# Splitting the second output projection of a tile in three, with the transposes of an earlier tile ahead of the last piece

## The chip, the cores and the metric

The kernel runs on one core of one Trainium2 chip. The metric is the device time of one execution in microseconds (us); the median of the runs is given. The core has five engines that matter here: TensorE (PE, matmuls and transposes), VectorE (DVE), ScalarE (ACT), GpSimd (POOL) and the queue of SyncE (SP), which issues nearly all DMAs.

## The reference, cut to what matters

A trunk of two layers works on two request groups (256 and 512 rows, D_MODEL = 1024). Each layer has a token mixer (layer 0: windowed attention with sinks; layer 1: differential attention) and a SwiGLU channel mixer, each between two RMS norms:

```python
for i in range(DEPTH):                        # DEPTH = 2
    h = rms_norm(x, norm_mix_pre[i])
    m = mixer(h)                              # ends with  o @ w_o   (1024 x 1024)
    x = x + rms_norm(m, norm_mix_post[i])
    h = rms_norm(x, norm_ffn_pre[i])
    x = x + rms_norm(swiglu(h, ffn_w_gate_up[i], ffn_w_down[i]), norm_ffn_post[i])
```

The change lies where a mixer ends and its SwiGLU begins: the product with `w_o`, the norm after it, the residual add, the norm before the SwiGLU, and the transposes that give the SwiGLU its operands. This place occurs twice, once in each layer.

## The kernel before, in words

The 768 rows are six tiles of 128 (0 and 1 are the prompt, 2 to 5 the sample). Every float32 product is made of three matmuls on a high and a low part (`product_steps`, L306; the matmuls are L315, L316 and L317; L316 and L317 need one low part each). The high part is an ACT copy, the low part a DVE subtraction: `split` (L303, L304) for activations, `two_parts` (L222, L223) for weights. Weights come through a ring of five split buffers; `free` and `take` (L291, L298) split the next unit as soon as a buffer is free, and issue the loads (`wraw`, L196, on SP's queue) behind it.

`project` (L737) makes the second 512 columns of the output projection. For a tile t, `out_unit` (L541) is a list of steps: eight products (k = 0 to 7, three matmuls each) into one PSUM bank, then `project_end` (L552): ACT squares and sums the bank (L559), DVE multiplies it by the gain into `o[t]` (L560). For tile 5, the last, four releases of weight buffers stand between the products, one after every second (`releasing`, L325), so its list has 13 entries and that of the others nine. `half` cuts the list in two pieces; both are called by `staged` (L499).

`staged` goes over the tiles in the order 0, 3, 1, 2, 4, 5. For a tile the four stages of `finish` (L458) follow its projection: a, the reciprocal root of the row norm (ACT L359, POOL L360); b, the residual add (DVE L472), the row norm of the sum (ACT L365, L359, POOL L360) and the store of x (SP, L476); c, the scaled tile y (DVE L369); d, `combine` (L420): eight transposes on PE (L433, bank tp_h) and the splits out of their banks (ACT L303, DVE L304). For tiles 0, 1 and 2, stage d splits the two banks and copies them to `o` (ACT L442). For tiles 3, 4 and 5 it also forms the operands s1 to s4 of the SwiGLU's Strassen-like product (L447 to L457), which makes eight DVE and five ACT instructions. In an iteration the order is: first piece of the tile's projection, stage c of the tile two steps before, stage b of the tile one step before, second piece, stage d of the tile two steps before, stage a of the tile itself. Stages a to c are issued with high priority.

The five stages that are left over for tiles 4 and 5 are called by `ffn` (L940), in the order c of 4, b of 5, two products (`p1`, L963, bank px), d of 4, more products (p2), c of 5, two more p1, d of 5, and so on; then p4 (bank pz), p6 (py, with s2), p5 (pw, with s1). The first px matmul reads the high part of tiles 0, 1 and 2, the second (L316) their low part. The combinations of gate and up weights (L257 to L261) run on DVE from there on.

The order in which an engine runs its instructions is fixed when the program is built: the tile framework orders by priority (the order of the calls above, high priority first) among the instructions whose inputs it expects to be ready. In the trace each engine's instructions stand in the order of its list.

Of the kernel before, what the change touches and what calls it, by code (L numbers as in the profile page):

```python
# [19 lines left out]
KT = D // P  # L20
# [11 lines left out]
NT = 6  # L32
# [14 lines left out]
def trunk(  # L47
# [93 lines left out]
    raw_src, units = [], []  # L141
# [149 lines left out]
    def take(n):  # L291

        i = state["used"]
        state["used"] += n
        prepare(i + n)
        return [parts.pop(j) for j in range(i, i + n)]
# [97 lines left out]
    def load_x(sub, t):  # L394
        x = xpool.tile([P, D], F32, tag="x", name=f"x{sub}_{t}")
        nc.sync.dma_start(out=x, in_=x_at[sub][t])
        return x
# [60 lines left out]
    def finish(sub, t, o, ssy, x, g, comb):  # L458

        r = {}
        m, (ss, y) = o[t], ssy

        def stage_a():
            with tc.high_priority():
                r[0] = rstd(ss[:, 1:2], ss[:, 0:1], f"post{sub}_{t}")

        def stage_b():  # L470
            with tc.high_priority():
                state["add"] = nc.vector.scalar_tensor_tensor(  # L472
                    out=x, in0=m, scalar=r[0], in1=x, op0=ALU.mult, op1=ALU.add)
                if g is not None:
                    r[1] = row_rstd(x, y, f"pre{sub + 1}_{t}")
            nc.sync.dma_start(out=x_at[sub + 1][t], in_=x)  # L476

        def stage_c():
            with tc.high_priority():
                scaled(y, x, r[1], g)  # L480

        def stage_d():
            if comb is not None:
                combine(y, t, f"h{sub + 1}_{t}", comb, o)
                return
            for s in transposes(y, t, f"h{sub + 1}_{t}"):
                s()

        return [stage_a, stage_b] + ([stage_c, stage_d] if g is not None else [])

    def last_tile(sub, t, m, ssy, x, r):

        halves = [slice(0, 512), slice(512, 1024)]
        for c, q in zip(halves, (nc.sync, nc.scalar)):
            nc.vector.scalar_tensor_tensor(
                out=x[:, c], in0=m[:, c], scalar=r, in1=x[:, c], op0=ALU.mult, op1=ALU.add)
            q.dma_start(out=x_at[sub + 1][t][:, c], in_=x[:, c])

    def staged(sub, units, o, sq, g, comb=None):  # L499

        st = []
        for i, t in enumerate((0, 3, 1, 2, 4, 5) if comb is not None else range(NT)):
            x = load_x(sub, t)
            units[t][0]()
            if i >= 2 and g is not None:
                st[i - 2][2]()
            if i >= 1:  # L510
                st[i - 1][1]()
            units[t][1]()
            if i >= 2 and g is not None:
                st[i - 2][3]()
            if g is None and t == NT - 1:
                last_tile(sub, t, o[t], sq[t], x, sq["last"])
                break
            st.append(finish(sub, t, o, sq[t], x, g, comb))
            st[i][0]()
        if g is None:  # L520
            return []
        return [st[NT - 2][2], st[NT - 1][1], st[NT - 2][3], st[NT - 1][2], st[NT - 1][3]]
# [15 lines left out]
    def column_blocks(taken, width):  # L538
        return [tuple(w[:, j * width:(j + 1) * width] for w in s) for s in taken for j in range(2)]

    def out_unit(t, wk, o, n2, gp, sq, name):  # L541

        pm = bank(name)
        steps = product_steps(pm, [(htile(t, k), wk[k]) for k in range(KT)])
        if t == NT - 1:
            steps = releasing(steps, 4)
        return steps + [lambda: project_end(t, pm, o, n2, gp, sq, name)]  # L550
# [16 lines left out]
    def mixer_a(gp, g_next, first_steps, o):  # L567
        with ExitStack() as st:
# [164 lines left out]
            for s in att[:2] + fill[:2] + att[2:4] + fill[2:4] + att[4:] + fill[4:6] + [lambda: split_o(NT - 1)] + fill[6:]:  # L733
                s()
        return project(o, 0, 0, None, gp, g_next, wk_o, sq, LAG + 1)

    def project(o, layer, sub, turn_o, gp, g_next, wk, sq, done):  # L737
        gs = ExitStack()
        gpool2 = gs.enter_context(tc.tile_pool(name=f"comb{layer}", bufs=1, side="right", reuse_waits="tile"))
        comb = {  # L740
            n: tuple(gpool2.tile([P, 4, HALF], F32R, name=f"{n}{part}_{layer}") for part in ("hi", "lo"))
            for n in ("s1", "s2", "s4")}
        for t in range(done, NT):
            if turn_o is not None and t + 1 < NT:
                for s in turn_o(t + 1):
                    s()
            for s in out_unit(t, wk, o, 0, gp, sq, f"po{layer}_0_{t}"):
                s()
        wk = column_blocks(take(4), 512)
        units = {}  # L750
        for t in range(NT):
            steps = []

            def half(i, t=t, steps=steps):
                if i == 0:
                    steps += out_unit(t, wk, o, 1, gp, sq, f"po{layer}_1_{t}")
                n = len(steps) // 2
                for s in (steps[:n] if i == 0 else steps[n:]):
                    s()

            units[t] = [lambda half=half: half(0), lambda half=half: half(1)]
        return staged(sub, units, o, sq, g_next, comb), comb, gpool2, gs


    def mixer_b(gp, g_next, first_steps, o):
        with ExitStack() as st:
# [168 lines left out]
            for s in run:  # L935
                s()
        return project(o, 1, 2, lambda t: turn_o[t][1:], gp, g_next, wk_o, sq, 3)


# [539 lines left out]
```

## Time and profile before

| | us |
|---|---|
| median of 3 runs | 1687.86 |
| lowest and highest run | 1686.98, 1690.11 |
| the profiled execution's own time | 1688.34 |
| its span, first to last instruction | 1686.6 |
| PE busy in it | 1659.1 (98%) |
| DVE, ACT, POOL busy | 1251.3, 949.7, 81.7 |

The time of the profiled execution exceeds its span by 1.7 us, which lie around the instructions. Times in the rows count from the start of the span. The stage of layer 0 lies at about 262 to 341 us, that of layer 1 at about 1155 to 1234 us. The granted clock (PEclk) is TensorE's clock as a share of full speed; its mean over the span is 0.997.

### The profile page before, as it was taken

What the parts mean: (1) busy time and instruction counts of PE and PEld (TensorE: products, weight loads), DVE (VectorE), ACT (ScalarE), POOL (GpSimd) and SP (SyncE); (2) the same over time, 40 slices, a digit from 0 to 9 for tenths busy, and PEclk for the clock granted to TensorE, in tenths of its full rate; (3) what the DMA queues carried; (4) which work ended last, traced back from release to release, by engine and by line L of the source; (5) the groups of instructions that cost most, each with busy time, mean ns of one, the idle gap of its engine ahead of it and who ended that gap; (6) DMA issues with size and microseconds to landing.
All of it is one profiled execution on the core that took longest, in us unless ns stands there. A gap on an engine that the chain in (4) does not pass through costs nothing. (4 is left out here: it accounts for less than half of the span.)

```text
span 1686.6 us, 25513 instructions
## 1 busy us (share of the span) xinstructions
PE 1659.1 (98%) x9483; PEld 1514.3 (90%) x9483; DVE 1251.3 (74%) x2488; ACT 949.7 (56%) x2158; POOL 81.7 (5%) x104
## 2 busy tenths in 40 slices
PE   7999999999999999999999999999899999999998
PEld 7888878899999998888999999988799999998887
DVE  7888766896766666988777676874997666666886
ACT  6777775654444444556566666674744444444553
POOL 1000001000000000001000000331000000000001
PEclk9999999999999999999999999999999999999999
DMA  6111014534333347666211111113444343336765
GB/s 212 39 38 48 14 38 150 175 134 140 109 125 99 128 139 250 230 235 205 83 39 38 38 38 38 48 51 113 170 138 141 108 141 108 128 114 226 249 222 176
DMA packets 62107, 207.30 MB, mean 123 GB/s; under 512 B 6752, under 2 KB 8928, under 8 KB 61728
## 3 DMA queue, kind: packets, MB, share of 16 engines
q1 hardware_dynamic: 55152, 175.15, 30.8%
q0 software_dynamic: 6688, 30.28, 5.6%
q8 instruction: 74, 1.21, 0.3%
q14 instruction: 49, 0.40, 0.1%
q10 hardware_dynamic: 144, 0.26, 0.0%
HBM read 162.80 MB, written 42.86 MB: 122 GB/s over the span
## 5 line engine op out<-in xcount | busy, mean ns | idle before, releaser
L223 DVE TENSOR_TENSOR wlo<-wraw,whi 128x1024 fp32r<-128x1024 f32 (+2 forms) x180 | 204.9, 1144 | 173.9 <-ACT whi L222 172.7
L222 ACT CAST whi<-wraw 128x1024 fp32r<-128x1024 f32 (+2 forms) x180 | 176.5, 986 | 117.4 <-PE py L316 58.9
L315 PE MATMUL py<-hhi,whi 128*128 128x384 f32 x464 | 155.4, 335 | 0.8 <-ACT u L976 0.8
L317 PE MATMUL py<-hhi,wlo 128*128 128x384 f32 x464 | 155.0, 334 | 0.0
L316 PE MATMUL py<-hlo,whi 128*128 128x384 f32 x464 | 155.0, 334 | 0.0
L315 PE MATMUL pqb<-whi,hhi 128*128 128x384 f32 x384 | 136.5, 356 | 0.0
L316 PE MATMUL pqb<-wlo,hhi 128*128 128x384 f32 x384 | 128.9, 336 | 0.0
L317 PE MATMUL pqb<-whi,hlo 128*128 128x384 f32 x384 | 128.8, 335 | 0.0
L303 ACT CAST hhi<-araw 128x768 fp32r<-128x768 f32 (+1 forms) x74 | 57.6, 783 | 94.6 <-DMA araw<-act 94.2
L317 PE MATMUL pv<-whi,hlo 128*128 128x512 f32 (+1 forms) x240 | 92.2, 384 | 0.4 <-DVE hlo L304 0.4
L315 PE MATMUL pv<-whi,hhi 128*128 128x512 f32 (+1 forms) x240 | 92.4, 385 | 0.0
L316 PE MATMUL pv<-wlo,hhi 128*128 128x512 f32 (+1 forms) x240 | 92.1, 384 | 0.0
L304 DVE TENSOR_TENSOR hlo<-araw,hhi 128x768 fp32r<-128x768 f32 (+1 forms) x74 | 65.2, 889 | 32.3 <-ACT hhi L303 32.1
L315 PEld LDWEIGHTS py<-hhi,whi 128*128 128x128 f32 x464 | 87.1, 188 | 1.7 <-ACT u L976 1.4
L316 PEld LDWEIGHTS py<-hlo,whi 128*128 128x128 f32 x464 | 87.1, 188 | 0.0
L317 PEld LDWEIGHTS py<-hhi,wlo 128*128 128x128 f32 x464 | 87.1, 188 | 0.0
L315 PE MATMUL po<-whi,hhi 128*128 128x512 f32 x192 | 77.9, 406 | 0.2 <-ACT hhi L303 0.2
L317 PE MATMUL po<-whi,hlo 128*128 128x512 f32 x192 | 75.4, 393 | 0.2 <-DVE hlo L304 0.2
L316 PE MATMUL po<-wlo,hhi 128*128 128x512 f32 x192 | 75.3, 392 | 0.0
L315 PEld LDWEIGHTS pqb<-whi,hhi 128*128 128x128 f32 x384 | 72.3, 188 | 2.0 <-issue 1.7
L315 PE MATMUL pqa<-whi,hhi 128*128 128x384 f32 x192 | 73.9, 385 | 0.0
L315 PE MATMUL px<-hhi,whi 128*128 128x384 f32 x208 | 70.8, 342 | 2.7 <-ACT hhi L303 2.7
(303 smaller groups left out, 4829.6 us busy)
## 6 DMA issues: line engine op xcount, KB each, us to landing
act<-st POOLq DMA_DIRECT2D x22, 1344.0 KB, 6.6
wraw<-in_wgu SPq DMA_DIRECT2D x56, 512.0 KB, 4.6
araw<-act SPq DMA_DIRECT2D x70, 384.0 KB, 4.0
y_wraw<-in_wgu SPq DMA_DIRECT2D x40, 512.0 KB, 3.6
wraw<-in_wd SPq DMA_DIRECT2D x40, 512.0 KB, 3.9
wraw<-in_wb SPq DMA_DIRECT2D x32, 384.0 KB, 3.2
xd<-x SPq DMA_DIRECT2D x18, 512.0 KB, 3.0
x<-xd SPq DMA_DIRECT2D x18, 512.0 KB, 4.1
```

The costliest lines, as they stand in the source:

```text
L222: state["raw_hi"] = nc.scalar.copy(out=hi, in_=src)
L223: state["raw_lo"] = nc.vector.tensor_tensor(out=lo, in0=src, in1=hi.bitcast(F32), op=ALU.subtract)
L303: state["hi"] = nc.scalar.copy(out=hi, in_=src)
L304: state["lo"] = nc.vector.tensor_tensor(out=lo, in0=src, in1=hi.bitcast(F32), op=ALU.subtract)
L315: nc.tensor.matmul(out, ah, bh, start=start and i == 0, stop=False, skip_group_check=more)
L316: nc.tensor.matmul(out, ah, bl, start=False, stop=False, skip_group_check=more)
L317: nc.tensor.matmul(out, al, bh, start=False, stop=stop and i == last, skip_group_check=more)
```

## The change

`half` cuts the list of steps into three pieces in place of two, and `staged` calls the third one after stage d of the tile two steps before. The cuts are at 4 and 6 for a list of nine entries (products 0 to 3; products 4 and 5; products 6 and 7 with `project_end`), and at 4 and 8 for the 13 of tile 5 (products 0 to 2 with one release; products 3 to 5 with one release; two releases, products 6 and 7, `project_end`). Before, they were at 4 and at 6. Nothing else changes; the same instructions are issued.

```diff
@@ staged
             units[t][1]()
             if i >= 2 and g is not None:
                 st[i - 2][3]()
+            units[t][2]()
             if g is None and t == NT - 1:
@@ project
             def half(i, t=t, steps=steps):
                 if i == 0:
                     steps += out_unit(t, wk, o, 1, gp, sq, f"po{layer}_1_{t}")
-                n = len(steps) // 2
-                for s in (steps[:n] if i == 0 else steps[n:]):
+                cut = (0, KT // 2, 3 * KT // 4 + (2 if t == NT - 1 else 0), len(steps))
+                for s in steps[cut[i]:cut[i + 1]]:
                     s()
 
-            units[t] = [lambda half=half: half(0), lambda half=half: half(1)]
+            units[t] = [lambda half=half, i=i: half(i) for i in range(3)]
```

## Rows read from the trace of the kernel before

**Rows 1.** The page, busy time of each engine, its share of the span.

```profile
PE 1659.1 (98%) x9483; PEld 1514.3 (90%) x9483; DVE 1251.3 (74%) x2488; ACT 949.7 (56%) x2158; POOL 81.7 (5%) x104
```

**Rows 2.** Waits of PE over the span: releaser, total us, times, longest.

```profile
PE px L315 <- ACT hhi L303: 2.7, 2, 1.4
PE py L316 <- DVE s2lo L304: 2.3, 2, 1.7
PE px L316 <- DVE hlo L304: 1.8, 2, 1.1
PE pz L315 <- ACT whi L222: 1.5, 2, 0.8
```

**Rows 3.** Timeline, layer 0: start, length, instruction, idle before it and releaser.

```profile
295.72 0.39 PE L315 MATMUL po<-whi,hhi 128*128 128x512 f32 x1
...
297.09 1.03 PE L433 MATMUL tp_h<-ident,y_po 128*128 128x128 f32 x8
...
298.28 0.59 ACT L559 ACTIVATE y_po<-po 128x512 f32<-128x512 f32 x1
298.46 0.57 POOL L360 TENSOR_TENSOR rstd_pre<-rstd_pre,mhalf 128x1 f32<-128x1 f32 x1 [4.15 <-ACT rstd_pre L359]
...
298.85 0.59 ACT L303 CAST hhi<-tp_h 128x512 fp32r<-128x512 f32 x1
...
299.07 1.28 DVE L369 SCALAR_TENSOR_TENSOR y_po<-x,rstd_pre,gpre 128x1024 f32<-128x1024 f32 x1 [0.44 <-POOL rstd_pre L360]
...
299.49 0.62 PE L315 MATMUL px<-hhi,whi 128*128 128x384 f32 x2 [1.37 <-ACT hhi L303]
...
299.71 1.05 POOL L360 TENSOR_TENSOR rstd_post<-rstd_post,mhalf 128x1 f32<-128x1 f32 x1 [0.67 <-ACT rstd_post L359]
...
300.41 1.30 PE L433 MATMUL tp_h<-ident,y_po 128*128 128x128 f32 x8 [0.30 <-DVE y_po L369]
...
302.01 0.68 DVE L304 TENSOR_TENSOR hlo<-tp_h,hhi 128x512 fp32r<-128x512 f32 x1
...
302.60 1.27 DVE L472 SCALAR_TENSOR_TENSOR x<-oa,rstd_post,x 128x1024 f32<-128x1024 f32 x1
302.74 0.69 PE L316 MATMUL px<-hlo,whi 128*128 128x384 f32 x1 [0.71 <-DVE hlo L304]
```

**Rows 4.** Windows, the px products of layers 0 and 1; PEclk third from last.

```profile
303.20:308.00 4.80, 4.80 (x16) 4.80 (x16) 3.01 (x5) 3.01 (x7) 0.55 (x1) 0.50 0.90 284
1196.20:1201.00 4.80, 4.80 (x29) 4.80 (x28) 4.70 (x6) 3.43 (x8) 0.55 (x1) 1.00 0.80 258
```

**Rows 5.** Timeline of DVE, layer 0, behind the projection of tile 4.

```profile
290.20 1.28 DVE L369 SCALAR_TENSOR_TENSOR y_po<-x,rstd_pre,gpre 128x1024 f32<-128x1024 f32 x1 [0.45 <-POOL rstd_pre L360]
...
293.82 0.68 DVE L560 TENSOR_TENSOR oa<-po,gpost 128x512 f32<-128x512 f32 x1
294.42 0.68 DVE L304 TENSOR_TENSOR hlo<-tp_h,hhi 128x512 fp32r<-128x512 f32 x1
295.01 1.27 DVE L472 SCALAR_TENSOR_TENSOR x<-oa,rstd_post,x 128x1024 f32<-128x1024 f32 x1
```

**Rows 6.** Timeline of PE and DVE, later in both stages, to the last wait.

```profile
308.00 1.28 DVE L369 SCALAR_TENSOR_TENSOR y_po<-x,rstd_pre,gpre 128x1024 f32<-128x1024 f32 x1 [1.79 <-POOL rstd_pre L360]
...
324.60 0.69 DVE L258 TENSOR_TENSOR wraw<-wraw,wraw 128x512 f32<-128x512 f32 x1 [0.84 <-DMA wraw<-in_wgu]
...
341.33 0.44 PE L315 MATMUL py<-hhi,whi 128*128 128x384 f32 x1 [0.30 <-ACT u L976]
...
1190.29 1.03 PE L433 MATMUL tp_h<-ident,y_po 128*128 128x128 f32 x8
...
1216.64 0.69 DVE L258 TENSOR_TENSOR wraw<-wraw,wraw 128x512 f32<-128x512 f32 x1 [1.29 <-DMA wraw<-in_wgu]
...
1218.48 0.68 DVE L304 TENSOR_TENSOR s2lo<-y_po,s2hi 128x512 fp32r<-128x512 f32 x1
...
1233.58 0.44 PE L315 MATMUL py<-hhi,whi 128*128 128x384 f32 x1 [0.51 <-ACT u L976]
```

## The prediction, made before the changed kernel had run

> **What bounds the kernel now.** I read the page first: PE is busy for 1659.1 of 1686.6 us [rows 1], so only PE's 27.5 idle us, and time in which it runs slowly, can be won. Next the list of PE's waits: the four longest that lie in the two stages of the change are for the high part of a tile (2.7 us), for s2lo (2.3), for a low part (1.8) and for a split weight (1.5), each once per layer [rows 2]. Nothing else in PE's work is touched.
>
> Then the timeline of layer 0 [rows 3]. PE goes through the projection without a gap until the transposes of tile 2 at 297.09. They are the last thing it has: its next work, the px products, needs tile 2 split. It idles 1.37 us until ACT has the high part, runs two matmuls, waits 0.30 us for the y of tile 4, transposes that, and waits 0.71 us for the low part. That is 2.38 us per layer, about 5.1 us for both. Behind it TensorE's granted clock falls in layer 0: in 4.80 us it starts 16 matmuls at 0.50, where layer 1 starts 29 at 1.00 after nearly the same gap [rows 4]. The missing 13, at 4.80/29 = 0.166 us, are 2.2 us.
>
> Last I asked what paces the end of each stage. From the transposes of tile 2 to the last wait, layer 0 takes 341.33 - 297.09 = 44.24 us and layer 1 1233.58 - 1190.29 = 43.29 us, with the same instructions [rows 3, 6]. The slow clock that lost 2.2 us has cost 0.95 by then: the rest was made up, because PE meets a chain on DVE and the DMAs (the combinations L258 wait 0.84 and 1.29 us for their weights, s2lo stands behind them), whose end hardly depends on when PE arrives [rows 6].
>
> **The change, part by part.**
>
> *Two products move behind the transposes.* For tile 5 the transposes of tile 2 now go in front of six matmuls. The first of those six started at 295.72, so the transposes start 297.09 - 295.72 = 1.37 us earlier [rows 3]. Their input is there: the y of tile 2 was begun at 290.20 and takes 1.28 us [rows 5]. The three earlier iterations have the same pattern with as much slack, and PE has no gap there: worth nothing while PE has products to run. The 1.37 us equal the first gap, but I don't credit it in full: ACT runs its list in order, and the high part at 298.85 stood behind the square L559 at 298.28, which now comes after it; 298.85 - 298.28 = 0.57 us is sure, the rest depends on ACT's queue. The low part gains more: before, it began at 302.01, behind the y of tile 4 at 299.07; now it can go into the 0.44 us for which DVE idled before that y [rows 3]. Then the third gap (0.71 and up to 1.1 us) goes. At this place I expect PE to be ahead by between 0.57 + 0.71 = 1.3 us and the whole 2.4 us in each layer.
>
> *project_end moves behind stage d.* Its bank is finished later by the eight transposes (1.03 us at most) [rows 3], and its DVE multiply now stands behind the splits of the other tile. For tile 4 the multiply was at 293.82, one low part behind it at 294.42, then the add at 295.01 [rows 5]. Now up to two low parts of about 0.6 us of issue each come before the multiply; the add, which needs it, is up to 0.6 us later in layer 0 and at most 1.2 us if a third split slips in. From the add hangs the y of tile 4. I take +0.3 us on that chain per layer: DVE does the same work, and the 0.44 us of idle before that y is the cover. Without the cover the price is 1.2 us per layer.
>
> *Cuts and releases of tile 5.* The first cut lies one product earlier, and the last two releases come behind stage d. The stages called there are of high priority anyway, and the loads that the releases issue on SP wait for DVE to finish a raw buffer, not for their place in the queue: nothing. If that cover is gone, a weight is late by the one product, 0.68 us, half of the 1.37. No wait, DMA or instruction is added; SP's stores of x keep their order.
>
> *What is late next.* PE arrives earlier at py's L316 and pz, which wait for s2lo and a split weight. DVE had hardly any idle time before them, so the gain is given back there but for what DVE's own list gains: the 0.84 and 1.29 us for which L258 waited for weights can now hold s2lo (0.6 us of issue), since its tile is transposed earlier [rows 6]. That is 0.6 us per layer at best; with the +0.3 above I take 0.3 net.
>
> *The clock.* With less than half of the idle time left, I expect the fall in layer 0 not to happen; by the comparison of the layers that gives 0.95 us. It is not more, since the DVE chain then bounds layer 0 as it does layer 1.
>
> **Sum:** 0.95 + 2 x 0.3 = 1.55 us, on the profiled execution 1688.34 - 1.55 = 1686.8. The median of the runs is 0.48 us lower, at 1687.86, so 1686.3 there. The ends for unknown parts: up to 5.1 + 2.2 = 7.3 us won if nothing is given back; 2 x 1.2 = 2.4 us lost if the late multiplies bind in both layers. I take the value near the lower end of the gains since the nearest row, layer 0's lost 2.2 us of which 0.95 was left, says that over half is given back.
>
> One rule is weighed here. POOL's one-column power took 0.57 us beside an idle DVE and 1.05 us beside DVE's y and weight split, which read two SBUF operands [rows 3]. The Trainium skill (SBUF — State Buffer, Who interferes with whom) says that a DVE instruction with two SBUF inputs locks GpSimd's reads out for its whole length, while one with a single SBUF input doesn't. It speaks against the change if DVE's gap before the y of tile 4 is filled by a weight split rather than by a low part out of PSUM: each power then takes 0.48 us more, and the sum would be 1.55 - 0.96 = 0.6 us. I keep 1.55, as the filler I expect is the low part.
>
> **Rivals.**
>
> *All is kept.* If DVE's list is reordered well, with s2lo ahead of the weights, the wait behind doesn't grow. Then the 5.1 us of gaps are won, 1687.9 - 5.1 = 1682.8, and 1680.6 with the clock. For it: the framework orders afresh, and DVE idles 0.84 to 1.29 us behind DMAs. Against: those DMAs are issued only when DVE has read earlier weights. Chance 0.22.
>
> *Nothing is won.* PE's wait moves whole to s2lo and pz, and the clock still falls in one stage: 1687.9, give or take 0.5. For it: in layer 1 the clock held over the same gap, so the rows don't show a rule by which it will hold; DVE is the chain. Chance 0.20.
>
> *Slower.* The multiply of project_end behind the splits delays the add of tile 4, its y, and with it tile 5's. It decides where the delay exceeds the 0.44 us of idle: 1.2 us per layer, and if PE's gap moves so that the clock falls in layer 1 too, another 0.95: 1687.9 + 2.4 + 0.95 = 1691.2. Against: the px products fill PE meanwhile. Chance 0.07, of which 0.03 beyond 0.2%.
>
> The change could also fail to do what it says, were the transposes not placed earlier by the framework; the y's are ready 4 us ahead, so I give that nothing of its own: it is the second rival.
>
> **How the numbers follow.** The forecast, a gain of 0.5 to 3.4 us, has 0.51. A measurement of this kernel can tell about 0.2%, 3.4 us (the three runs shown lie 3.1 us apart). Faster by more than that is the first rival, 0.22. Slower by more is 0.03. The rest, 0.75, is the same. The range reaches down to 1682.5, just beyond the first rival without the clock, and up to 1689.5, 1.6 us above no change, short of the slower rival's full price; it leaves out about 0.1 below and 0.06 above.
>
> **What would show it.** Right: the transposes of tile 2 some 1.4 us earlier against the end of the projection; px's first wait under 0.9 us and its wait for the low part gone; px at full clock in layer 0; py's L316 waiting longer for s2lo, or pz for whi. The multiply L560 of tile 4 should stand behind two low parts. Wrong: waits at s2lo and whi no longer than now (then the first rival), px still at half clock, or a y of tile 4 later by over 1 us.

## The result, and the profile after

The changed kernel is slower. Its median is 1693.05 us (1691.01 to 1695.82), beside 1689.41 us (1686.98 to 1693.49) for the kernel before on the same chip: a ratio of 1.0023 [1.0015, 1.0030], the brackets being a 95% interval. (Here and below the ratio is an estimate of its own from the runs of both kernels; the quotient of the two medians differs from it by up to 0.0009.) I had forecast 1686.3 and a range that ended at 1689.5. The profiled execution took 1693.2 us with a span of 1691.4, 4.8 us more than before.

First the page's busy times, then PE's waits (releaser, total us, times, longest) of the changed kernel. Line numbers behind L515 are one higher than before.

```profile
PE 1659.7 (98%) x9483; PEld 1513.4 (89%) x9483; DVE 1251.2 (74%) x2488; ACT 949.7 (56%) x2158; POOL 78.3 (5%) x104
```

```profile
PE tp_h L433 <- DVE y_po L369: 5.4, 2, 2.8
PE py L316 <- DVE s2lo L304: 3.4, 2, 1.7
PE pz L315 <- ACT whi L222: 1.9, 2, 1.0
PE pz L316 <- DVE hlo L304: 1.5, 2, 1.2
...
PE py L315 <- ACT s2hi L303: 0.5, 2, 0.2
...
PE px L316 <- DVE hlo L304: 0.2, 1, 0.2
```

No engine has more work: PE's busy time grew by 0.6 us [rows 1], so 4.2 of the 4.8 us are waits. Of px's 4.5 us [rows 2] 0.2 are left, as the change meant. But the transposes L433 wait 4.8 us longer for a y (5.4 for 0.6), the first pz product 1.5 us for a low part that it did not wait for before, and s2lo, s2hi and whi take 1.1 + 0.5 + 0.4 us more. The sum of these, 8.3 - 4.3 = 4.0 us, is nearly the whole idle time gained.

The timeline of layer 0 where [rows 3] were, in the changed kernel:

```profile
297.16 1.29 DVE L369 SCALAR_TENSOR_TENSOR y_po<-x,rstd_pre,gpre 128x1024 f32<-128x1024 f32 x1 [0.71 <-POOL rstd_pre L360]
...
298.50 1.97 PE L433 MATMUL tp_h<-ident,y_po 128*128 128x128 f32 x8 [2.67 <-DVE y_po L369]
...
299.56 2.35 DVE L223 TENSOR_TENSOR wlo<-wraw,whi 128x1024 fp32r<-128x1024 f32 x2
...
300.12 0.78 PE L315 MATMUL po<-whi,hhi 128*128 128x512 f32 x1
...
301.83 0.68 DVE L304 TENSOR_TENSOR hlo<-tp_h,hhi 128x512 fp32r<-128x512 f32 x1
302.03 0.55 POOL L360 TENSOR_TENSOR rstd_pre<-rstd_pre,mhalf 128x1 f32<-128x1 f32 x1 [4.39 <-ACT rstd_pre L359]
302.16 0.51 PE L315 MATMUL px<-hhi,whi 128*128 128x384 f32 x2
...
302.62 1.28 DVE L369 SCALAR_TENSOR_TENSOR y_po<-x,rstd_pre,gpre 128x1024 f32<-128x1024 f32 x1
```

The y of tile 2 now begins at 297.16, where it began at 290.20 [rows 5]. So its transposes, which I expected at about 295.72, start at 298.50, and the six matmuls of tile 5 (two products) that could have run stand behind them on PE's queue. The gap ahead of px has become a gap of 2.67 us in the middle of the projection; layer 1 has the same one, of 2.77.

Where in the program is it lost? Take the start of tile 0's y (DVE L369) in each layer as a zero; it lies ahead of the first instruction that the change moves. Before, the zeros are 272.54 and 1165.67, after 272.49 and 1168.31. From layer 0's zero to layer 1's the time grew by 895.82 - 893.13 = 2.69 us, from there to the end of the span by 523.09 - 520.93 = 2.16. That is one execution of each: among the kernels below that lose nothing measurable, the first time lies between 891.2 and 894.6 us and the second between 520.6 and 523.6. So this split does not settle how much each layer loses; that both have the same delays is in the table at the end of the experiments.

Next, the iteration of **tile 1** in layer 0, in which stage d of tile 0 is called; these are the first instructions that come late. The kernel before, ACT and DVE:

```profile
278.28 0.60 ACT L559 ACTIVATE y_po<-po 128x512 f32<-128x512 f32 x1 [0.85 <-PE po L317]
...
280.62 0.59 ACT L442 COPY oa<-tp_h 128x512 f32<-128x512 f32 x1 [0.50 <-DVE hlo L304]
```

```profile
279.30 0.68 DVE L560 TENSOR_TENSOR oa<-po,gpost 128x512 f32<-128x512 f32 x1
279.90 0.68 DVE L304 TENSOR_TENSOR hlo<-tp_h,hhi 128x512 fp32r<-128x512 f32 x1
280.50 1.27 DVE L472 SCALAR_TENSOR_TENSOR x<-oa,rstd_post,x 128x1024 f32<-128x1024 f32 x1
...
284.29 1.28 DVE L369 SCALAR_TENSOR_TENSOR y_po<-x,rstd_pre,gpre 128x1024 f32<-128x1024 f32 x1 [1.91 <-POOL rstd_pre L360]
```

And the changed kernel, ACT and then DVE:

```profile
277.31 1.07 ACT L303 CAST hhi<-tp_h 128x512 fp32r<-128x512 f32 x2
279.96 0.59 ACT L442 COPY oa<-tp_h 128x512 f32<-128x512 f32 x1 [1.58 <-DVE hlo L304]
280.45 0.60 ACT L560 ACTIVATE y_po<-po 128x512 f32<-128x512 f32 x1
```

```profile
278.04 1.28 DVE L369 SCALAR_TENSOR_TENSOR y_po<-x,rstd_pre,gpre 128x1024 f32<-128x1024 f32 x1 [2.23 <-POOL rstd_pre L360]
279.25 1.28 DVE L304 TENSOR_TENSOR hlo<-tp_h,hhi 128x512 fp32r<-128x512 f32 x2
281.17 0.69 DVE L561 TENSOR_TENSOR oa<-po,gpost 128x512 f32<-128x512 f32 x1 [0.64 <-ACT y_po L560]
282.47 1.28 DVE L472 SCALAR_TENSOR_TENSOR x<-oa,rstd_post,x 128x1024 f32<-128x1024 f32 x1 [0.61 <-POOL rstd_post L360]
285.99 1.28 DVE L369 SCALAR_TENSOR_TENSOR y_po<-x,rstd_pre,gpre 128x1024 f32<-128x1024 f32 x1 [2.23 <-POOL rstd_pre L360]
```

The transposes of tile 0 come 1.4 us earlier, so ACT's list now has both high parts and the first copy ahead of the square of tile 1. The copy starts only when the low part of the same bank is done on DVE, and DVE is at the y of tile 3. ACT stands still for 1.58 us with the square behind the copy; the multiply waits for the square, the norm for the square too, and the add of tile 1 starts at 282.47 for 280.50, its y at 285.99 for 284.29.

Last, the chain of work that ended last, layer 1 (start us, us, what). The kernel before, and then the changed one:

```profile
1194.64 0.60 DVE ob L560
...
1195.76 1.27 DVE x L472
1197.04 1.15 DVE wlo L223
...
1198.20 4.44 DMA wraw<-in_wgu
...
1211.17 3.93 DMA wraw<-in_wgu
```

```profile
1168.31 1.29 DVE y_po L369
...
1175.04 0.61 DVE hlo L304
...
1175.67 0.59 ACT ob L442
1176.26 0.59 ACT y_po L560 x2
...
1178.18 1.30 DVE x L472
...
1189.02 1.29 DVE x L472
...
1194.08 1.28 DVE x L472
1195.35 1.15 DVE wlo L223
1196.52 5.01 DMA wraw<-in_wgu
...
1216.27 5.25 DMA wraw<-in_wgu
```

In both, the chain ends this stage the same way: an add, a weight's low part, the load that this sets free, and on to the weights' combination (L258), twice. In the changed kernel it can be followed further back, through the low parts of tile 0 (1175.04), the add of tile 1 (1178.18), the add of tile 2 (1189.02) and the add of tile 4 (1194.08). The chain of the kernel before breaks off at 1194.64, so it does not tell whether it came through these adds as well; that of "tiles 2, 4 and 5" below, which has no measurable loss, does. What the changed kernel's chain has and that one's has not is the piece between the low part and the add of tile 1: the copy (1175.67), the square (1176.26) and the norm stand in it, 2.5 us, where in "tiles 2, 4 and 5" the add follows the low part directly (1172.78 + 0.55, then 1173.33). The second combination, at 1216.64 before [rows 6], stands here:

```profile
1221.62 0.69 DVE L258 TENSOR_TENSOR wraw<-wraw,wraw 128x512 f32<-128x512 f32 x1 [1.17 <-DMA wraw<-in_wgu]
```

From the zero that is 53.31 us for 50.97; in layer 0 it is 53.79 for 52.06.

### The profile page after: what moved, and what is told of

Read it like the earlier page. It is cut to its first block, busy times and chain, and to the rows that moved or that the text cites. A ratio compares the mean times of both kernels' runs of the same rounds, so it can differ in the third digit from the quotient of the medians.

```text
span 1691.4 us, 25512 instructions
## 1 busy us (share of the span) xinstructions
PE 1659.7 (98%) x9483; PEld 1513.4 (89%) x9483; DVE 1251.2 (74%) x2488; ACT 949.7 (56%) x2158; POOL 78.3 (5%) x104
## 4 chain that ended last, share of the span: by engine, by line
PE 79%; DVE 7%; DMA 6%; ACT 3%; issue 3%; POOL 1%; SPq 0%; DVEq 0%; ACTq 0%; POOLq 0%
PE py L315 6%; PE py L316 6%; PE py L317 6%; PE pw L315 4%; PE pw L316 4%; PE pw L317 4%; PE pqb L315 4%; PE pqb L316 4%; PE pqb L317 4%; PE pob L872 2%; PE pv L317 2%; PE pv L316 2%; PE pv L315 2%; PE px L317 2%; PE px L316 2%
## 5 line engine op out<-in xcount | busy, mean ns | idle before, releaser
L316 PEld LDWEIGHTS pqb<-wlo,hhi 128*128 128x128 f32 x384 | 72.4, 188 | 0.6 <-DVE wlo L223 0.5
```

The source lines that it names most:

```text
L316: nc.tensor.matmul(out, ah, bl, start=False, stop=False, skip_group_check=more)
```

## The experiments

The letters in the expectations: **A**, the loss is the multiply of tile 2, which now stands behind the eight DVE instructions of tile 3's combine (add of tile 2 at 293.37 for 286.69). **B**, it is tile 5's own list and its releases. **C**, each late `project_end` has a share. **D**, it is tile 1's iteration, as above. **E**, the late pieces of several tiles add up. All kernels were timed beside the kernel before; ratios are to that. Adds, y's and combinations are counted from the zero of their layer.

The edit for "late for some tiles only", with `late` the tiles whose third piece comes behind stage d; the others have two pieces, as before:

```diff
             units[t][1]()
+            if t not in late:
+                units[t][2]()
             if i >= 2 and g is not None:
                 st[i - 2][3]()
-            units[t][2]()
+            if t in late:
+                units[t][2]()
...
+                n = len(steps) // 2
-                cut = (0, KT // 2, 3 * KT // 4 + (2 if t == NT - 1 else 0), len(steps))
+                cut = (0, KT // 2, 3 * KT // 4 + (2 if t == NT - 1 else 0), len(steps)) if t in late else (
+                    0, n, len(steps), len(steps))
```

**Tile 5 only** (`late = (5,)`).

> Only tile 5 has three pieces with stage d ahead of the last one; the other tiles are as before. Theory A (the loss comes from the iteration of tile 2: its multiply L560 stands behind the eight DVE instructions of tile 3's combine, so tile 2's add and y come some 7 us later): no loss, 0 to 2.5 us faster than before, y of tile 2 ready some 4 us ahead of its transposes, PE's first wait for px under 0.9 us. Theory B (the loss comes from tile 5's own list: the last two releases, and with them the loads of gate weights, stand behind stage d): 2.5 to 4 us slower, as the whole change. Theory C (each delayed project_end adds its share): about 1 us slower.

Measured: 1688.55 beside 1689.01, 0.9997 [0.9988, 1.0007]. PE's queue in layer 0:

```profile
296.36 1.03 PE L433 MATMUL tp_h<-ident,y_po 128*128 128x128 f32 x8
...
299.60 0.62 PE L315 MATMUL px<-hhi,whi 128*128 128x384 f32 x2 [0.84 <-ACT hhi L303]
...
301.10 1.09 PE L433 MATMUL tp_h<-ident,y_po 128*128 128x128 f32 x8 [0.88 <-DVE y_po L369]
...
302.84 0.44 PE L316 MATMUL px<-hlo,whi 128*128 128x384 f32 x1 [0.46 <-DVE hlo L304]
```

```profile
PE py L316 <- DVE s2lo L304: 4.0, 2, 2.4
```

This is the part that I had priced. The first wait is 0.84 us for 1.37 and the third 0.46 for 0.71 [rows 3], but the transposes wait 0.88 for 0.30, and s2lo takes 4.0 us for 2.3 [rows 2]. The transposes come 1.5 us earlier against the zero, as forecast (23.08 for 24.55). The kernel neither gains nor loses; B falls.

**Tile 2 only** (`late = (2,)`).

> Only tile 2 has three pieces (stage d there is tile 3's combine); tile 5 and the others are as before. A: all of the loss or more, 3 to 7 us slower than before, since the transposes of tile 2 don't have tile 5's last products behind them; the y of tile 2 begins some 7 us later against the projection than before. B: within 1 us of before. C: about 1 us slower.

Measured: 1689.87 beside 1689.01, 0.9999 [0.9990, 1.0008]. The y of tile 2 comes at 23.09 us for 17.66, and nothing is lost: alone, it isn't A.

**The whole change, with `project_end` of the second half at high priority.**

```diff
-            nc.scalar.activation(out=junk, in_=pm, func=AF.Square, ...)
-            nc.vector.tensor_tensor(...)
+            with tc.high_priority() if n2 else ExitStack():
+                nc.scalar.activation(out=junk, in_=pm, func=AF.Square, ...)
+                nc.vector.tensor_tensor(...)
```

> The whole change, with the square and the multiply of project_end (second half only) issued at high priority, so that DVE takes the multiply of tile 2 between two instructions of tile 3's combine. A: the loss goes; 0 to 3 us faster than before, PE's wait for y of tile 2 under 0.5 us. B: still 3 to 4 us slower, since the releases stand where they stood. C: the loss goes too, as all multiplies move.

Measured: 1693.12 beside 1689.01, 1.0024 [1.0015, 1.0034]. The y of tile 2 is back to 21.27 us from 24.67, and the loss is what it was. But the add of tile 1 is still at 10.01, since its square stands behind the copy as before.

**Tiles 1, 4 and 5** (`late = (1, 4, 5)`).

> Three pieces for tiles 1, 4 and 5, not for tile 2 (and not for 0 and 3, which have no stage d in their iteration). A: no loss, within 0 to 2.5 us faster than before. B: 2.5 to 4 us slower. C: 2 to 3 us slower, three quarters of the whole.

Measured: 1695.29 beside 1689.01, 1.0032 [1.0019, 1.0045], without tile 2. A, which expected no loss here, falls. The next two kernels part tile 1 from the rest.

**Tile 1 only** (`late = (1,)`).

> Only tile 1 has three pieces (its stage d is tile 0's). Theory D (the loss starts in tile 1's iteration: its square on ACT stands behind a copy that waits for DVE, its add comes 2 us later, DVE idles meanwhile, and as DVE is busy from then on to the last add of the stage, the 2 us are not made up): 3 to 4.5 us slower than before, the y of tile 5 begins 1.5 to 3 us later against the y of tile 0 than before, in both layers. Theory E (it takes the late pieces of tiles 4 and 5 together with tile 1's, since neither loses alone): under 1 us slower. Theory C (each late project_end a share): about 1 us slower.

Measured: 1693.43 beside 1690.34, 1.0021 [1.0012, 1.0031]. One iteration per layer loses as much as the whole change; C and E, which expected about 1 us and under 1 us, fall. ACT's gap is that of the changed kernel:

```profile
280.13 0.59 ACT L442 COPY oa<-tp_h 128x512 f32<-128x512 f32 x1 [1.58 <-DVE hlo L304]
280.61 0.60 ACT L563 ACTIVATE y_po<-po 128x512 f32<-128x512 f32 x1
```

The add and the y of tile 1 come at 10.01 and 13.53 us, for 7.96 and 11.75. From that y to the add of tile 5 this kernel takes 31.84 - 13.53 = 18.31 us, and the kernel before 30.06 - 11.75, the same; DVE idles 0.88 us in it in both. So the delay of 1.8 us is handed on whole.

**Tiles 2, 4 and 5** (`late = (2, 4, 5)`), the whole change but for tile 1.

> Three pieces for tiles 2, 4 and 5, not for tile 1. D: no loss, within 1.5 us of before on either side, add of tile 1 at its old place 7.9 us after the y of tile 0. E: between 0 and 2 us slower. C: 2 to 3 us slower.

Measured: 1691.98 beside 1690.34, 1.0007 [0.9998, 1.0016]. This fits D, and E's 0 to 2 us as well; it is the run of tile 1 alone, where E expected under 1 us, that speaks for D.

**Tile 5 only, and the kernel before, each with `project_end` at high priority.** I tried whether an earlier multiply makes a faster kernel.

> Three pieces for tile 5 alone, with project_end's square and multiply (second half) at high priority, which puts tile 5's multiply on DVE ahead of a weight split of 1.1 us. If the end of the stage is set by the chain from tile 5's add to its y, the loads and the split weights (D's reading), the add comes 1 to 2 us earlier than with three pieces for tile 5 alone, and the kernel is 1 to 4 us faster than before. If the end is set by DVE's total of work alone, it is within 1 us of before.

> The kernel before with only the high priority of project_end's square and multiply. If the chain from tile 5's add sets the end of the stage: 1 to 3 us faster than before. If DVE's total does: within 1 us of before.

Measured: 0.9995 [0.9987, 1.0004] and 1.0004 [0.9994, 1.0015]. In both the add of tile 5 comes 0.6 us earlier (29.5 for 30.1), and nothing is won: a miss. Being early there does not pay.

**Tile 1, with all eight products ahead of stage d and only `project_end` behind it** (`late = (1,)`, and another cut).

```diff
-                cut = (0, KT // 2, 3 * KT // 4 + (2 if t == NT - 1 else 0), len(steps)) if t in late else (
+                cut = (0, KT // 2, KT, len(steps)) if t in late else (
```

> Tile 1 alone; all eight products of its second half stay ahead of stage d of tile 0, and only the square and the multiply (its project_end) are written behind stage d. On every engine the order comes out as in the kernel before: ScalarE has the square ahead of the first hi part, VectorE the multiply ahead of the first lo part. Theory D (the loss is tile 1's square standing on ScalarE behind a copy that waits for VectorE, which in turn needs the transposes ahead of the products on TensorE): add of tile 1 at 7.9 to 8.0 us after y of tile 0, its y at 11.7, ratio to before 0.999 to 1.001. Rival (the mere place of the square and the multiply in the program behind stage d costs the time): ratio 1.0015 or more, as with tile 1's whole third piece (1.0021).

Measured: 1688.07 beside 1689.84, 0.9994 [0.9983, 1.0004]. ACT's and DVE's lists in this stage are those of the kernel before, so their place in the program costs nothing by itself where the lists don't change. What is left is that the transposes overtake the products and that ACT's list turns round with them; the next kernel parts these two.

**Tile 1 only, with tile 0's copies behind the square.** PE's order is that of "tile 1 only".

```diff
-                nc.scalar.copy(out=o[t][:, b * 512:(b + 1) * 512], in_=tp)
+                copy = lambda b=b, tp=tp: nc.scalar.copy(out=o[t][:, b * 512:(b + 1) * 512], in_=tp)
+                if state.get("defer"):
+                    copies.append(copy)
+                else:
+                    copy()
...
+                state["defer"] = t in (1,)
-                st[i - 2][3]()
+                copies = st[i - 2][3]() or []
...
             units[t][2]()
+            for c in copies:
+                with tc.issue_after(state["square"].ins):
+                    c()
```

> Tile 1 alone with three pieces, as in the run that lost 0.21%; but ScalarE's two copies of tile 0 (the transposed tile into oa) are put behind tile 1's square, so that the square no longer stands behind a copy that waits for the second lo part on VectorE. The multiply is still behind both lo parts. Theory D: the square starts about 1.4 us earlier (as soon as TensorE's last product is done, some 0.8 us later than in the kernel before), the add of tile 1 comes about 1.0 us earlier than with the copy ahead: 8.8 to 9.1 us after y of tile 0 (7.96 before, 10.01 with the copy ahead), y of tile 1 at 12.3 to 12.6 (11.75 and 13.53); so a loss of about 0.7 to 1.0 us for each of two layers in place of 1.8 to 2.0: ratio 1.0007 to 1.0014. Rival (the earlier transposes themselves or the lo parts ahead of the multiply are the loss, the copy is not): ratio 1.0018 to 1.0025, whatever the add does.

Measured: 1688.80 beside 1689.84, 1.0000 [0.9991, 1.0009]. ACT and DVE:

```profile
278.46 0.60 ACT L574 ACTIVATE y_po<-po 128x512 f32<-128x512 f32 x1 [0.68 <-PE po L317]
...
279.41 0.59 ACT L443 COPY oa<-tp_h 128x512 f32<-128x512 f32 x1 [0.25 <-DVE hlo L304]
```

```profile
280.85 1.29 DVE L477 SCALAR_TENSOR_TENSOR x<-oa,rstd_post,x 128x1024 f32<-128x1024 f32 x1 [0.28 <-POOL rstd_post L360]
```

The zero of this kernel is 271.98, so the add comes at 8.87 us, as worked out ahead, and no loss can be told (by the interval at most 0.09%); I had expected a third to two thirds of it to stay. So, with tile 1 alone, the copy ahead of the square is the loss, and the 0.6 us by which the add of tile 5 is still late cost nothing measurable.

**The whole change with the copies of tiles 0, 1 and 2 behind the squares.** The same edit on the changed kernel, in all its iterations:

```diff
+                state["defer"] = t in (1, 2, 4, 5)
```

> The whole change, with stage d's two ScalarE copies of tiles 0, 1 and 2 put behind the square of the iteration in which they stand. Theory D: tile 1's add at 8.8 to 9.1 us after y of tile 0 in place of 9.98, its y at 12.3 to 12.6 in place of 13.50; of the change's 0.23% about half remains: ratio 1.0008 to 1.0015. Rival (the loss is spread over all iterations, or the copies do not matter): ratio 1.0020 to 1.0030.

Measured: 1692.83 beside 1689.84, 1.0027 [1.0017, 1.0037]. Nothing comes back. By D alone half of it should have: D is right for tile 1, but is not all of the change.

**The whole change, and tiles 1, 4 and 5, with tile 0's copies alone behind tile 1's square** (`t in (1,)` again; the second with `late = (1, 4, 5)`).

> The whole change, with only tile 0's two ScalarE copies put behind tile 1's square (in the run before, the copies of tiles 1 and 2 were moved as well, and nothing came back). Theory D' (tile 1's delay is what costs; what moving the copies of tiles 1 and 2 did gave it back): tile 1's y at 12.3 to 12.5 us after y of tile 0, the second combination of the FFN's weights (its DMA wait) at 51.2 to 52.3 us (51.5 before, 53.6 with the whole change), ratio 1.0003 to 1.0014. Theory E (tile 1's remaining 0.64 us and the late pieces of tiles 2, 4 and 5 together cost what tile 1's 1.8 us cost alone): second combination at 53 to 54 us, ratio 1.0020 to 1.0030, as in the run that moved all the copies.

> Late third pieces for tiles 1, 4 and 5 and not for tile 2 (1.0032 as that stood), with tile 0's copies behind tile 1's square. Theory D': second combination of the FFN's weights at 51.2 to 52.3 us after y of tile 0 (54.15 as it stood), ratio 1.0000 to 1.0012. Theory E, with the late pieces of tiles 4 and 5 as what adds up with tile 1's 0.64 us: 53 to 54 us, ratio 1.0018 to 1.0030. If this one is back and the whole change with the same edit is not, tile 2's late piece is what adds up.

Measured: 1.0022 [1.0014, 1.0031] and 1.0015 [1.0006, 1.0025]. By the first D' falls; the second, 1.0032 with the copy ahead, lies between the two theories. In these the y of tile 1 is early (12.5), and the add of tile 5 is still late: 31.48 and 31.00 for 30.06. Between tile 1 and the rest, the delays of that add are nearly a sum: tiles 2, 4 and 5 make it 0.7 us (30.77), tile 1 with the square first 0.6 (30.71), both together 1.4 (31.48); tile 1 with the copy ahead 1.8 (31.84), and the whole change 2.6 (32.70). Among tiles 2, 4 and 5 they are not: tile 2 alone has 0.6 and tile 5 alone 1.2, but the three together 0.7. That these delays add up is theory F of the last two.

**The whole change with the priorities and with tile 1's square first; the whole change with the priorities and all of tile 1's products ahead of stage d.** The first joins the edits shown above; the second has the priorities and

```diff
-                cut = (0, KT // 2, 3 * KT // 4 + (2 if t == NT - 1 else 0), len(steps))
+                cut = (0, KT // 2, KT if t == 1 else 3 * KT // 4 + (2 if t == NT - 1 else 0), len(steps))
```

> The whole change with both repairs: tile 0's copies behind tile 1's square, and the squares and multiplies of the second half at high priority. Theory F (each edit's delay of tile 5's residual add is added up, a delay of up to about 0.8 us there costs nothing and what lies beyond it is lost in each layer): add of tile 5 at 30.6 to 30.9 us after y of tile 0 (30.1 before; 32.6 with the whole change; 31.8 with the priorities alone, of which 1.1 is the copy's), ratio 0.9993 to 1.0009. Rival E' (the late third pieces of tiles 1, 2, 4 and 5 together cost the time by themselves, however early the adds are): ratio 1.0015 to 1.0030, the second combination of the FFN's weights at 53 us or later.

> The whole change with the priorities, and with all eight products of tile 1 ahead of stage d, so that tile 1 is as in the kernel before. Theory F: add of tile 5 at 29.9 to 30.3 us after y of tile 0, ratio 0.9990 to 1.0006. Rival E': 1.0007 to 1.0025, as tiles 2, 4 and 5 are still late.

Measured: 1.0015 [1.0006, 1.0024] and 0.9999 [0.9989, 1.0008]. The second loses nothing measurable with tiles 2, 4 and 5 late, so E' falls. In the first the add of tile 5 came about where it was expected (30.92 and 30.75), but 1.0015 lies outside F's range: F as I wrote it, with 0.8 us free, falls too.

All kernels together, us from the zero, layer 0 / layer 1:

| kernel | add of tile 1 | add of tile 5 | second combination | ratio |
|---|---|---|---|---|
| before | 7.96 / 7.88 | 30.06 / 30.09 | 52.06 / 50.97 | 1 |
| tile 5 | 7.91 / 7.85 | 31.22 / 31.14 | 51.39 / 51.59 | 0.9997 |
| tile 2 | 7.96 / 7.85 | 30.69 / 30.63 | 51.72 / 51.70 | 0.9999 |
| tiles 2, 4, 5 | 7.97 / 7.85 | 30.77 / 30.72 | 51.22 / 51.42 | 1.0007 |
| tile 1, end only | 7.98 / 7.84 | 30.08 / 29.99 | 51.23 / 50.98 | 0.9994 |
| all, priority, tile 1's products ahead | 7.99 / 7.85 | 30.27 / 30.12 | 51.62 / 50.89 | 0.9999 |
| tile 1, square first | 8.87 / 8.81 | 30.71 / 30.58 | 51.37 / 51.09 | 1.0000 |
| all, priority, square first | 8.93 / 8.80 | 30.92 / 30.75 | 52.29 / 52.06 | 1.0015 |
| tiles 1, 4, 5, square first | 8.93 / 8.81 | 31.00 / 30.82 | 52.29 / 53.64 | 1.0015 |
| all, square of 1 first | 8.95 / 8.82 | 31.48 / 31.35 | 53.21 / 52.27 | 1.0022 |
| all, squares first | 8.88 / 8.82 | 31.42 / 31.36 | 54.15 / 53.43 | 1.0027 |
| tile 1 | 10.01 / 9.89 | 31.84 / 31.66 | 53.26 / 52.99 | 1.0021 |
| all, priority | 10.01 / 9.88 | 31.86 / 31.66 | 53.47 / 53.57 | 1.0024 |
| the change | 9.98 / 9.87 | 32.70 / 32.40 | 53.79 / 53.31 | 1.0023 |
| tiles 1, 4, 5 | 10.01 / 9.89 | 32.09 / 31.89 | 54.18 / 54.12 | 1.0032 |
| tile 5, priority | 7.97 / 7.85 | 29.49 / 29.46 | 52.41 / 52.87 | 0.9995 |
| before, priority | 7.97 / 7.85 | 29.47 / 29.46 | 53.51 / 52.55 | 1.0004 |

No kernel is measurably faster than the one before. Whatever tiles 2, 4 and 5 do, a kernel with tile 1's products ahead of the transposes loses nothing that can be told; with them behind, every kernel loses 0.15% or more but the one that has nothing else late and the square first. For the late add of tile 5 the steps are not in proportion: 0.6 us cost nothing, 0.7 us 0.07% (not told from nothing), 0.8 us 0.15%, 1.3 to 2.5 us cost 0.21 to 0.32%; as each ratio is known to some 0.1%, neighbouring steps can't be told apart. "Tile 5" is an exception (1.1 us, no loss). The last two rows are exceptions of the other kind, a late combination that costs nothing. Both kinds fit better at the y of tile 5, the last one. From the zero, as the mean of both layers, it comes at 33.5 to 35.5 us in the kernels without a measurable loss ("tile 5" 35.0, "tile 5, priority" 33.5, "before, priority" 33.5), and at 35.4 to 37.2 in those with one ("all, priority, square first" 35.6, the change 36.8). This was sought out afterwards among several such times, so it is a hint and not a cause shown; what keeps the loss in the whole change once the square is first stays open.

## Why the prediction was wrong

**The step that failed** is "The three earlier iterations have the same pattern with as much slack, and PE has no gap there: worth nothing while PE has products to run". PE has no gap there, that is right. But the iteration of tile 1 alone, to which I gave no cost, takes the ratio to 1.0021, and without it no loss can be told (1.0007 [0.9998, 1.0016]). I looked at PE, the busiest engine, and at whether the transposes' input was ready; I didn't lay ACT's and DVE's lists of that iteration side by side. The transposes in front of two products put ACT's two high parts and a copy ahead of the square, and the copy waits for DVE (1.58 us). The add of tile 1 is 2.0 us later, its y 1.7 us. DVE idles only 0.88 us from that y to the add of tile 5, too little to take it back. Shown is the place, tile 1's iteration, and for tile 1 alone the copy ahead of the square; in the whole change, putting the square first brought nothing back (1.0022) and with the priorities at most a part (1.0015 for 1.0024), so there the copy is not the only cause.

**The second is a size.** For `project_end` behind stage d I took +0.3 us per layer on the chain of tile 4, at most 1.2. I priced it for tile 4 alone, "the 0.44 us of idle before that y is the cover". It can arise in each iteration: the add of tile 5 is 2.6 and 2.3 us late. For tile 2 I had not reckoned that stage d is tile 3's combine, nine DVE instructions (the kernel in words says eight) and not two: its multiply stands behind eight of them (291.99), and PE then waits for that tile's y at the very transposes that were to start 1.37 us earlier.

**What is late next** was right in kind. I wrote that PE meets a chain on DVE and the DMAs whose end hardly depends on when PE arrives. In the tile 5 kernel 1.7 us of the gain came back at s2lo, and nothing was won, as in my second rival. What I missed is the other side of that sentence: if the end hangs on DVE's chain, then what delays DVE can be paid. The chain suggests how a delay is passed on: the load for the next weights is issued when DVE has read the earlier ones (1195.35, then 5.01 us of DMA). It is not shown that this is what costs the time: "before, priority" has its second combination 1.5 us later and loses nothing measurable.

**The slower rival** had the mechanism, a multiply behind splits, but the wrong place (tile 4), and a chance of 0.07. It gave 1691.2, 3.3 us above the kernel before, and 3.6 us were measured (1693.05 and 1689.41). That the sizes agree is luck: 0.95 us of the 3.3 were for the clock, and the rest for another place.

**The clock** did not stay up in the profiled execution. The windows around the projection's end (us, busy PE, PEld, DVE, ACT, POOL, then the granted clock, DMA share, GB/s), layer 0, then layer 1:

```profile
295.50:298.50 3.00, 0.33 (x2) 0.00 (x1) 2.29 (x4) 3.00 (x8) 1.06 (x2) 0.91 0.43 173
298.50:301.50 3.00, 3.00 (x12) 2.77 (x13) 3.00 (x3) 2.39 (x5) 0.00 (x0) 0.52 0.64 214
301.50:304.00 2.50, 2.50 (x14) 2.16 (x13) 2.40 (x4) 1.91 (x6) 1.03 (x2) 1.00 0.94 241
```

```profile
1196.00:1198.30 2.30, 2.14 (x7) 1.33 (x5) 2.30 (x4) 1.91 (x7) 0.74 (x1) 0.50 0.93 333
```

And the px products of layer 0 in "tile 1, end only", whose ACT and DVE lists here are those of the kernel before:

```profile
302.67:307.47 4.80, 4.80 (x29) 4.80 (x29) 4.70 (x6) 3.44 (x8) 0.55 (x1) 1.00 0.92 279
```

In layer 0 the slow stretch is shorter than before and ends ahead of px; in layer 1, which had none there [rows 4], there is one. But the term of 0.95 us had no ground to begin with: I took it from the difference of the two layers in one execution. In "tile 1, end only" the clock stays at 1.00 in both layers behind gaps of 1.36 and 0.30 us, where in the kernel before it fell to 0.50 behind 1.37 and 0.30; and there the stretch that I had measured takes 43.49 us in layer 0 and 44.54 in layer 1, a difference of 1.05 us the other way with no fall at all. Nor is the clock the loss: "all, square of 1 first" loses 0.22%, and its profiled execution (1692.70 us) has 1.00 over this place in both layers.

**The rule that I weighed** had next to no part. The two weight splits did come into DVE's place before the y of tile 4 (299.56), the order that I had not expected, but the power for that y ran in layer 0 beside a low part out of PSUM, in 0.55 us (302.03). That agrees with the Trainium skill (SBUF — State Buffer, Who interferes with whom), by which a DVE instruction with at most one SBUF input, outside the 2-port modes, does not contend with GpSimd. In layer 1 the power began under the end of the second split and took 0.74 us, 0.19 more; the 0.96 us that I had worked out for this order did not arise.

**The points to look for** came out mixed: px's waits gone, px at full clock in layer 0 and tile 4's multiply behind two low parts (295.76 behind 294.56), as forecast; the transposes of tile 2 later and not earlier; py's and pz's waits longer; the y of tile 4 at 30.13 us for 26.53, which I had named as a sign that the forecast is wrong.

## What to carry to other kernels

If a step is moved ahead on the busiest engine, write down the lists of the engines that consume it, at every place where it moves, those without a gap too: what has come forward may put an instruction that waits ahead of one that does not. Where a chain on a second engine ends the stage, slack on the first says little about the price. And when undoing one cause brings nothing back, look at the delays at a late point of the chain before dropping the cause: another edit may keep the chain as late. Whether the delays add up there has to be tried; here they did between tile 1 and the rest, and not among the rest.

## What the runs showed that I had not expected

Where ACT stood idle ahead of it, a copy on ACT out of a PSUM bank started just as DVE's low part of the same bank ended (279.96 behind 279.25 + 0.68; before 280.62 behind 279.90 + 0.68; with the square first 279.41, released by the same low part). Two readers of one bank stood in a row there. No run here tells whether the chip or the framework's order of the bank's readers wants that.

TensorE's clock was granted at 0.52, about its lower level of 1.2 of 2.4 GHz, behind a wait of 2.67 us at the transposes, and 3 us later it was back at 1.00. In layer 1 it was at 0.50 some 2 us behind a wait of 2.77 us, with PE running in between. With the same order of ACT and DVE and nearly the same gaps it fell in one execution (the kernel before, layer 0) and stayed at 1.00 in another ("tile 1, end only"). So from one trace of a kernel one can't tell that the next execution will have the fall.
